# Scaling rows inside the transposition: the first stage of a hybrid recurrence and sparse-attention block

## The chip, the core and the metric

The kernel runs on one core of one Trainium2 chip. The metric is device time in microseconds (us) of one execution; lower is better. One execution was also recorded by the hardware profiler, and its trace gives every instruction of every engine with its start and length: TensorE (PE, with the loading of its stationary operand as PEld), VectorE (DVE), ScalarE (ACT), GpSimd (POOL), and SyncE (SP), which issues most transfers. L12 stands for line 12 of the kernel.

## The reference

One layer of a streaming encoder over 512 tokens of width 2048, in float32. Only the head of it matters here:

```python
h = rmsnorm(x, norm_w[layer])          # x: (1, 512, 2048)
proj = h @ w_in[layer]                 # w_in: (2048, IN_WIDTH), split into eleven parts
(a_q, a_f, a_i, a_g, c_q, c_kv, k_idx_raw, w_idx_raw, b_g, m_a, m_b) = jnp.split(proj, SPLIT_POINTS, axis=-1)
y_a = hgrn2_branch(a_q, a_f, a_i, a_g, ...)      # gated linear recurrence, 8 heads of 128
y_b = dsa_branch(c_q, c_kv, k_idx_raw, ...)      # sparse attention over chosen keys
merged = sigmoid(m_a) * (y_a @ w_pa) + sigmoid(m_b) * (y_b @ w_pb)
out = rmsnorm(x + merged @ w_out, final_norm_w)
```

rmsnorm(x, w) is x times 1 / sqrt(mean(x * x) + 1e-6) of its row, times w by column. The factor of a row is one number for each token; w gives one number for each of the 2048 features.

## The kernel before

Products of float32 matrices are made from three products of rounded parts: each operand is split into a high part (rounded by ScalarE to the type fp32r) and a low part (the rest, subtracted by VectorE or GpSimd), and high x high, low x high and high x low are accumulated in one bank of PSUM. Nearly all of the span is such products, in jobs that follow one another on TensorE. The first of them can only start when the normalised input stands in SBUF with features on the partitions and tokens along the free axis, as xh (high) and xl (low). To make these is the first stage, the function start(). It also computes 272 of the columns of proj straight away: 256 columns of a_i (kept as v) and the 16 of w_idx_raw (kept as widx).

The order of the work is written out by hand: each engine runs its instructions in the order in which the program issues them, and waits by semaphores. ScalarE, VectorE, GpSimd and TensorE each work through one queue; SP's queue issues the loads of x (two halves for each tile of 128 tokens), of four groups of weights (raw[0] to raw[3], 512 rows by 272 columns each), of small rows, and of the first two weight tiles of the next stage (load_ahead).

The stage handles four tiles t of 128 tokens, each in four groups g of four 128 x 128 blocks. The names:

- turn (L309): 16 transpositions of tile t on TensorE by an identity, four to a bank of PSUM, pt.
- square and rstd (L298, L302): ScalarE sums the squares of the row's two halves, VectorE adds them, ScalarE takes the root. on_diag (L305): VectorE takes the reciprocal, the row factor, and puts it on a diagonal, diag. square, rstd and on_diag of tile t + 1 run within the work on tile t.
- spread (L337): a float32 matmul of an all-ones matrix by diag brings the factor of each token onto all partitions; VectorE copies it to SBUF as r (rrow).
- weigh (L317, tile 0 alone): the four blocks of a bank times the feature's weight wc, to ys[g]; then scaled (L398) multiplies by r. For tiles 1 to 3, scaled (L348) does both in four instructions for a group.
- high (L321) rounds ys[g] to xh[g] on ScalarE; low (L324) subtracts it on VectorE, for odd groups of tiles 1 to 3 on GpSimd.
- w_high and w_low (L329, L332): the same two parts of the group's weights, wh and wl (fh, fl in the profile); the low part of the last group is made on GpSimd.
- project (L371): the 48 products of a tile, 128 x 128 by 128 x 272, group by group; the next tile's follow (L344: turn, spread, the rows' work) is issued in the middle, after group 1, and the copies to v and widx at the end. In the last tile, prep(0), which splits the next stage's first weights, stands there instead.

Before the first transposition, TensorE runs four float32 matmuls of ones (L292) into a bank that nobody reads, and the transposition of the feature weights nw.

Of the kernel before, what the change touches and what calls it, by code (L numbers as in the profile page):

```python
# [26 lines left out]
F32 = mybir.dt.float32  # L27
FR = mybir.dt.float32r
AF = mybir.ActivationFunctionType
OP = mybir.AluOpType  # L30
# [4 lines left out]
T, D = 512, 2048  # L35
# [15 lines left out]
def hybrid_block(ctx, tc, x, norm_w, w_in, lb_table, gnorm_a, q_norm_w, kv_norm_w, w_uq,  # L51
# [3 lines left out]
    V, A, G, PE, SP = nc.vector, nc.scalar, nc.gpsimd, nc.tensor, nc.sync  # L55
# [7 lines left out]
    mmp = ctx.enter_context(tc.tile_pool(name="mmp", bufs=4, space=PSUM))  # L63
# [4 lines left out]
    def bank(name):  # L68
        return sdp.tile([128, 512], F32, name=name, tag="sd")
# [10 lines left out]
    def mm(ps, l, r, first, last):  # L80
        PE.matmul(ps, l, r, start=first, stop=last, skip_group_check=True)  # L81
# [168 lines left out]
    def start():  # L250
        R.v0 = enter("v0")
        p0 = enter("p0", side="right")
        ident = p0.tile([128, 128], F32, name="ident")
        A.dma_start(ident, c_ident)
        HF = D // 2
        nw = p0.tile([16, 128], F32, name="nw")
        wc = p0.tile([128, 16], F32, name="wc")
        xs = [[p0.tile([128, HF], F32, name=f"x{t}{i}") for i in range(2)] for t in range(4)]
        ys = [p0.tile([128, 4, 128], F32, name=f"y{g}") for g in range(4)]
        diag = p0.tile([128, 128], F32, name="diag")  # L260
        sq = p0.tile([128, HF], mybir.dt.bfloat16, name="sq")
        st = p0.tile([128, 4, 4], F32, name="st")
        rows = p0.tile([128, 128], F32, name="rows")
        G.memset(rows, 1.0)
        G.tensor_copy(ones_r, rows)
        wh = [p0.tile([128, 4, 272], FR, name=f"fh{i}") for i in range(4)]
        wl = [p0.tile([128, 4, 272], FR, name=f"fl{i}") for i in range(4)]
        raw = [None] * 4

        def load_x(t):  # L270
            for i in range(2):
                SP.dma_start(xs[t][i], x2[t * 128:(t + 1) * 128, i * HF:(i + 1) * HF])

        def load_w(i):
            raw[i] = p0.tile([128, 4, 272], F32, name=f"fr{i}")
            for o, c0, c1 in ((0, 2048, 2304), (256, 4992, 5008)):
                SP.dma_start(raw[i][:, :, o:o + c1 - c0],
                             w_in[i * 512:(i + 1) * 512, c0:c1].rearrange("(k p) n -> p k n", p=128))
# [12 lines left out]
        for _ in range(4):  # L291
            PE.matmul(warm[:, 0:128], ones, ones, start=True, stop=True)  # L292
        G.memset(rows, 0.0)
        pw = mmp.tile([128, T], F32, name="acc")
        PE.transpose(pw[:, 0:16], nw, ident[0:16, 0:16])
        V.tensor_copy(wc, pw[:, 0:16])

        def square(t, i):  # L298
            A.activation(sq, xs[t][i], AF.Square, accum_out=st[:, t, i:i + 1])

        def rstd(t):
            V.tensor_add(st[:, t, 2:3], st[:, t, 0:1], st[:, t, 1:2])  # L302
            A.activation(st[:, t, 2:3], st[:, t, 2:3], AF.Sqrt, bias=eps, scale=1.0 / D)

        def on_diag(t):  # L305
            V.reciprocal(st[:, t, 3:4], st[:, t, 2:3])
            V.tensor_scalar(diag, ident, st[:, t, 3:4], None, op0=OP.mult)

        def turn(t, g):  # L309
            pt = bank("pt")  # L310
            for j in range(4):
                k = g * 4 + j
                PE.transpose(pt[:, j * 128:(j + 1) * 128],
                             xs[t][k // 8][:, (k % 8) * 128:(k % 8) * 128 + 128], ident)
            return pt

        def weigh(pt, g):  # L317
            V.tensor_tensor(ys[g], pt.rearrange("p (j t) -> p j t", j=4),
                            wc[:, g * 4:g * 4 + 4, None].to_broadcast([128, 4, 128]), op=OP.mult)

        def high(t, g):  # L321
            A.activation(xh[g][:, :, t * 128:t * 128 + 128], ys[g], AF.Copy)

        def low(t, g):  # L324
            o = slice(t * 128, t * 128 + 128)
            (G if t and g % 2 else V).tensor_tensor(xl[g][:, :, o], ys[g], xh[g][:, :, o].bitcast(F32),
                                                    op=OP.subtract)

        def w_high(i):  # L329
            A.activation(wh[i], raw[i], AF.Copy)  # L330

        def w_low(i, eng):  # L332
            eng.tensor_tensor(wl[i], raw[i], wh[i].bitcast(F32), op=OP.subtract)

        v = hg[0, "v"] = R.v0.tile([128, 4, 256], F32, name="hv")

        def spread():  # L337
            pr = mmp.tile([128, T], F32, name="acc")
            PE.matmul(pr[:, 0:128], ones, diag, start=True, stop=True)
            r = p0.tile([128, 128], F32, name="rrow", bufs=2)  # L340
            V.tensor_copy(r, pr[:, 0:128])
            return r

        def follow(t):  # L344
            pts = [turn(t, g) for g in range(4)]
            r = spread()

            def scaled(g):  # L348
                for j in range(4):
                    V.scalar_tensor_tensor(ys[g][:, j, :], pts[g][:, j * 128:j * 128 + 128],  # L350
                                           wc[:, g * 4 + j:g * 4 + j + 1], r, op0=OP.mult, op1=OP.mult)
                high(t, g)

            scaled(0)
            scaled(1)
            low(t, 0)
            if t < 3:
                square(t + 1, 0)
            scaled(2)
            low(t, 1)  # L360
            if t < 3:
                square(t + 1, 1)
            scaled(3)
            if t < 3:
                rstd(t + 1)
            low(t, 2)
            if t < 3:
                on_diag(t + 1)
            low(t, 3)

        def project(t):  # L371
            o = slice(t * 128, t * 128 + 128)
            acc = mmp.tile([128, T], F32, name="acc")
            for g in range(4):
                if g == 2:
                    if t < 3:
                        follow(t + 1)
                    else:
                        prep(0)
                for n, (xp, wp) in enumerate(((xh, wh), (xl, wh), (xh, wl))):  # L380
                    for k in range(4):
                        mm(acc[:, 0:272], xp[g][:, k, o], wp[g][:, k, :], g + n + k == 0,
                           g + n + k == 8)
            A.activation(v[:, t, :], acc[:, 0:256], AF.Copy)
            V.tensor_copy(widx[:, t, :], acc[:, 256:272])

        pts = [turn(0, g) for g in range(4)]
        weigh(pts[0], 0)
        weigh(pts[1], 1)
        square(0, 0)  # L390
        square(0, 1)
        rstd(0)
        on_diag(0)
        w_high(0)
        weigh(pts[2], 2)
        r = spread()

        def scaled(g):  # L398
            V.tensor_tensor(ys[g], ys[g], r[:, None, :].to_broadcast([128, 4, 128]), op=OP.mult)
            high(0, g)  # L400

        scaled(0)
        scaled(1)
        w_low(0, V)
        w_high(1)
        low(0, 0)
        weigh(pts[3], 3)
        square(1, 0)
        scaled(2)
        low(0, 1)  # L410
        scaled(3)
        w_low(1, V)
        w_high(2)
        w_low(2, V)
        square(1, 1)
        low(0, 2)
        rstd(1)
        low(0, 3)
        on_diag(1)
        w_high(3)  # L420
        w_low(3, G)
        SP.dma_start(rows[0:16], lb_table.rearrange("a (h d) -> (a h) d", d=128))
        SP.dma_start(rows[16:20], q_norm_w.rearrange("o (k d) -> (o k) d", d=128))
        SP.dma_start(rows[20:22], kv_norm_w.rearrange("o (k d) -> (o k) d", d=128))
        SP.dma_start(rows[22:23], kidx_norm_w)
        SP.dma_start(rows[23:24], kidx_norm_b)
        SP.dma_start(rows[24:25], gnorm_a)
        load_ahead()
        for t in range(4):
            project(t)  # L430
        pt = bank("pt")
        PE.transpose(pt[:, :128], rows, ident)
        V.tensor_copy(cols[:, 0:25], pt[:, :25])
        leave("p0")
# [1122 lines left out]
```

## Time and profile before

| | |
|---|---|
| Times of three runs | 1369.58, 1370.32, 1370.65 us; median 1370.32 |
| Profiled execution: its span, first to last instruction | 1368.3 us; its own time is not given apart, the median of the runs is 2.0 us above this span |
| TensorE busy | 1347.3 us, 98% of the span |
| VectorE, ScalarE, GpSimd busy | 1072.6, 656.8, 83.2 us |
| First stage, on TensorE | from 1.38 to 46.77 us |

A busy figure is the time in which the engine had at least one instruction under way. A line of the timeline gives the start, the time from the first start to the last end of the instructions merged in it, the engine, the line of the kernel, the operation, out<-in by the program's names, the shape, the count, and in brackets the idle time before it with what ended it. A line of the waits gives the engine that waited and for what, the total, how often, and the longest.

### The profile page before, as it was taken

Reading aid. Unit: us, or ns where it says so; the run is one execution under the profiler, and the core shown is the slowest. Engines: PE = TensorE matmul, PEld = TensorE weight load, DVE = VectorE, ACT = ScalarE, POOL = GpSimd, SP = SyncE. Lnnn points to the kernel's source line nnn. Section 1 sums busy time; section 2 is a strip of 40 time slices with the busy share of each in tenths; the row PEclk is TensorE's granted clock in tenths of the full one; section 3 lists DMA queues with packets and bytes.
Section 4 is the critical chain, followed back from the end, with each engine's and each line's share of the span. In section 5 each row is a group of like instructions: output and inputs, shape, how many; then the busy total and the mean of one; then the engine's idle time right before and its main releaser. Section 6 shows DMA issues by size and latency. Waiting matters only on the chain. (4 is left out here: it accounts for less than half of the span.)

```text
span 1368.3 us, 26815 instructions
## 1 busy us (share of the span) xinstructions
PE 1347.3 (98%) x10940; PEld 1250.0 (91%) x10940; DVE 1072.6 (78%) x1743; ACT 656.8 (48%) x1054; POOL 83.2 (6%) x85
## 2 busy tenths in 40 slices
PE   8999999999999999999999999999999999999997
PEld 7888999999999999998999788878888888899996
DVE  7896889988898888876779989675556658899856
ACT  6555445545544444546744343645534334354435
POOL 2100000000000000000030303050101100000000
PEclk9999999999999999999999999999999999999999
DMA  6334345544454445446235423434856556643554
GB/s 206 93 109 138 107 141 170 155 139 140 139 148 126 116 138 152 144 139 200 63 103 149 130 79 109 137 104 144 285 179 203 197 172 221 208 150 113 171 201 168
DMA packets 144734, 204.79 MB, mean 150 GB/s; under 512 B 10538, under 2 KB 85987, under 8 KB 144483
## 3 DMA queue, kind: packets, MB, share of 16 engines
q1 hardware_dynamic: 144322, 202.75, 47.6%
q8 instruction: 86, 1.41, 0.4%
q14 instruction: 38, 0.30, 0.1%
q10 hardware_dynamic: 288, 0.33, 0.1%
HBM read 167.89 MB, written 35.15 MB: 148 GB/s over the span
## 5 line engine op out<-in xcount | busy, mean ns | idle before, releaser
L150 ACT ACTIVATE bh<-wr 128x768 fp32r<-128x768 f32 x128 | 108.2, 845 | 218.7 <-issue 108.2
L152 ACT ACTIVATE wh<-sv 128x512 fp32r<-128x512 f32 x256 | 151.8, 623 | 84.7 <-DVE sv L145 65.5
L73 DVE TENSOR_TENSOR wl<-wr,wh 128x1024 fp32r<-128x1024 f32 (+1 forms) x104 | 127.9, 1231 | 60.7 <-ACT wh L72 60.4
L76 PE MATMUL pp<-s,wh 128*128 128x256 f32 x624 | 172.3, 276 | 0.0
L77 PE MATMUL pp<-s,wh 128*128 128x256 f32 x624 | 172.3, 276 | 0.0
L78 PE MATMUL pp<-s,wl 128*128 128x256 f32 x624 | 172.3, 276 | 0.0
L153 DVE TENSOR_TENSOR bl<-wr,bh 128x768 fp32r<-128x768 f32 x128 | 122.3, 955 | 51.3 <-ACT bh L150 51.1
L72 ACT ACTIVATE wh<-wr 128x1024 fp32r<-128x1024 f32 (+1 forms) x104 | 108.1, 1040 | 113.1 <-PE acc L77 60.0
L154 DVE TENSOR_TENSOR wl<-sv,wh 128x1024 fp32r<-128x1024 f32 x128 | 156.5, 1223 | 7.4 <-ACT wh L152 1.1
L76 PE MATMUL acc<-xh,wh 128*128 128x512 f32 x304 | 121.6, 400 | 0.0
L78 PE MATMUL acc<-xh,wl 128*128 128x512 f32 x304 | 118.6, 390 | 0.0
L77 PE MATMUL acc<-xl,wh 128*128 128x512 f32 x304 | 118.4, 390 | 0.0
L77 PEld LDWEIGHTS pp<-s,wh 128*128 128x128 f32 x624 | 117.2, 188 | 0.0
L76 PEld LDWEIGHTS pp<-s,wh 128*128 128x128 f32 x624 | 117.1, 188 | 0.0
L78 PEld LDWEIGHTS pp<-s,wl 128*128 128x128 f32 x624 | 117.1, 188 | 0.0
L76 PE MATMUL pp<-xh,bh 128*128 128x256 f32 x416 | 114.9, 276 | 0.0
L78 PE MATMUL pp<-xh,bl 128*128 128x256 f32 x416 | 114.9, 276 | 0.0
L77 PE MATMUL pp<-xl,bh 128*128 128x256 f32 x416 | 114.9, 276 | 0.0
L76 PE MATMUL acc<-yh,wh 128*128 128x512 f32 x256 | 100.2, 391 | 0.0
L78 PE MATMUL acc<-yh,wl 128*128 128x512 f32 x256 | 99.8, 390 | 0.0
L77 PE MATMUL acc<-yl,wh 128*128 128x512 f32 x256 | 99.7, 390 | 0.0
L145 DVE TENSOR_TENSOR sv<-wr 128x512 f32<-128x512 f32 x128 | 87.9, 687 | 9.2 <-DMA wr<-in_w_in_dram 5.9
(390 smaller groups left out, 3688.4 us busy)
## 6 DMA issues: line engine op xcount, KB each, us to landing
wr<-in_w_in_dram SPq DMA_DIRECT2D x136, 512.0 KB, 3.7
wr<-in_w_out_dram SPq DMA_DIRECT2D x32, 512.0 KB, 3.7
mg<-gate_d SPq DMA_DIRECT2D x48, 256.0 KB, 5.0
gate_d<-c SPq DMA_DIRECT2D x44, 256.0 KB, 5.2
wr<-in_w_in_dram SPq DMA_DIRECT2D x36, 256.0 KB, 2.9
wr<-in_w_pa_dram SPq DMA_DIRECT2D x16, 512.0 KB, 5.7
wr<-in_w_pb_dram SPq DMA_DIRECT2D x16, 512.0 KB, 4.2
x<-in_x_dram SPq DMA_DIRECT2D x8, 512.0 KB, 4.2
```

The lines of the kernel that those rows point to most:

```text
L72: A.activation(hi, src, AF.Copy)
L73: V.tensor_tensor(lo, src, hi.bitcast(F32), op=OP.subtract)
L76: PE.matmul(ps, lh, rh, start=first, stop=False, skip_group_check=True)
L77: PE.matmul(ps, lh, rl, start=False, stop=False, skip_group_check=True)
L78: PE.matmul(ps, ll, rh, start=False, stop=last, skip_group_check=True)
L145: V.tensor_tensor(sv[:, 0:2, :], b[:, 1:3, :], b[:, 0:1, :].to_broadcast([128, 2, 256]), op=OP.add)
L150: A.activation(bh, b[:, 1:4, :], AF.Copy)
L152: A.activation(vh[:, i:i + 2, :], sv[:, i:i + 2, :], AF.Copy)
L153: V.tensor_tensor(bl, b[:, 1:4, :], bh.bitcast(F32), op=OP.subtract)
L154: V.tensor_tensor(vl, sv, vh.bitcast(F32), op=OP.subtract)
```

## The change

- The row factor goes into the transposition. turn multiplies each block of x, as the stationary operand, by diag of its tile in a float32 matmul, where a transposition by the identity stood. spread, rrow and the scaled functions are gone; weigh alone (one VectorE instruction for a group) serves all tiles, followed by the rounding to xh. There are two diag tiles.
- As turn now needs diag, the squares and the root of tile 0 stand ahead of turn(0).
- Twenty-six more float32 matmuls of ones stand on TensorE ahead of turn(0).
- All low parts, of x and of the weights, are made on VectorE.
- project and follow are replaced by use(t, parts), which issues the products of the named groups (hh, lh, hl: high x high, low x high, high x low) and, when a tile's twelve are issued, its copies to v and widx, and by rows_of(t), which issues the rows' work. The products of tiles 0 and 1 are ordered by hand across the two tiles.
- On ScalarE, w_high(2) and w_high(3) now come after the squares and the root of tile 1; on VectorE, w_low(2) and w_low(3) come after rows_of(1).

```diff
-        diag = p0.tile([128, 128], F32, name="diag")
+        diag = [p0.tile([128, 128], F32, name=f"diag{i}") for i in range(2)]
...
+        for _ in range(26):
+            PE.matmul(warm[:, 0:128], ones, ones, start=True, stop=True)
...
-            V.tensor_scalar(diag, ident, st[:, t, 3:4], None, op0=OP.mult)
+            V.tensor_scalar(diag[t % 2], ident, st[:, t, 3:4], None, op0=OP.mult)
+
+        pts, accs, done = {}, {}, {}
+
+        def turn(t):
+            for g in range(4):
+                pts[t, g] = bank("pt")
+                for j in range(4):
+                    k = g * 4 + j
+                    PE.matmul(pts[t, g][:, j * 128:(j + 1) * 128],
+                              xs[t][k // 8][:, (k % 8) * 128:(k % 8) * 128 + 128], diag[t % 2],
+                              start=j == 0, stop=True, skip_group_check=True)
+
+        def weigh(t, g):
+            V.tensor_tensor(ys[g], pts.pop((t, g)).rearrange("p (j t) -> p j t", j=4),
                             wc[:, g * 4:g * 4 + 4, None].to_broadcast([128, 4, 128]), op=OP.mult)
             A.activation(xh[g][:, :, t * 128:t * 128 + 128], ys[g], AF.Copy)
...
-            (G if t and g % 2 else V).tensor_tensor(xl[g][:, :, o], ys[g], xh[g][:, :, o].bitcast(F32),
-                                                    op=OP.subtract)
+            V.tensor_tensor(xl[g][:, :, o], ys[g], xh[g][:, :, o].bitcast(F32), op=OP.subtract)
...
+        def use(t, *parts):
+            if t not in accs:
+                accs[t], done[t] = mmp.tile([128, T], F32, name="acc"), 0
+            o = slice(t * 128, t * 128 + 128)
+            for kind, g in parts:
+                xp, wp = {"hh": (xh, wh), "lh": (xl, wh), "hl": (xh, wl)}[kind]
+                for k in range(4):
+                    mm(accs[t][:, 0:272], xp[g][:, k, o], wp[g][:, k, :], done[t] == 0 and k == 0, done[t] == 11)
+                done[t] += 1
+            if done[t] == 12:
+                A.activation(v[:, t, :], accs[t][:, 0:256], AF.Copy)
+                V.tensor_copy(widx[:, t, :], accs[t][:, 256:272])
+
+        def rows_of(t):
+            weigh(t, 0)
+            weigh(t, 1)
             low(t, 0)
             if t < 3:
                 square(t + 1, 0)
+            weigh(t, 2)
             low(t, 1)
             if t < 3:
                 square(t + 1, 1)
+            weigh(t, 3)
             if t < 3:
                 rstd(t + 1)
             low(t, 2)
             if t < 3:
                 on_diag(t + 1)
             low(t, 3)
...
         square(0, 0)
         square(0, 1)
         rstd(0)
         on_diag(0)
         w_high(0)
+        turn(0)
+        weigh(0, 0)
+        weigh(0, 1)
         w_high(1)
         low(0, 0)
+        weigh(0, 2)
+        low(0, 1)
+        weigh(0, 3)
         square(1, 0)
         square(1, 1)
         low(0, 2)
+        low(0, 3)
+        w_low(0)
         rstd(1)
         on_diag(1)
+        w_low(1)
+        w_high(2)
         w_high(3)
+        use(0, ("hh", 0), ("hh", 1), ("lh", 0), ("hh", 2), ("lh", 1), ("hh", 3), ("lh", 2), ("lh", 3))
+        turn(1)
+        use(0, ("hl", 0), ("hl", 1))
+        rows_of(1)
+        w_low(2)
+        w_low(3)
...
         load_ahead()
-        for t in range(4):
-            project(t)
+        use(1, ("hh", 0), ("hh", 1), ("lh", 0), ("hl", 0), ("hh", 2), ("lh", 1), ("hl", 1), ("hh", 3), ("lh", 2),
+            ("lh", 3))
+        turn(2)
+        use(0, ("hl", 2), ("hl", 3))
+        use(1, ("hl", 2), ("hl", 3))
+        rows_of(2)
+        for t in (2, 3):
+            use(t, *((kind, g) for g in (0, 1) for kind in ("hh", "lh", "hl")))
+            if t == 2:
+                turn(3)
+                rows_of(3)
+            else:
+                prep(0)
+            use(t, *((kind, g) for g in (2, 3) for kind in ("hh", "lh", "hl")))
```

More of the change, by code (lines that the diff above doesn't have):

```diff
@@ L306, in on_diag @@
             V.reciprocal(st[:, t, 3:4], st[:, t, 2:3])
[L307 to L318, printed above, removed]
+            V.tensor_scalar(diag[t % 2], ident, st[:, t, 3:4], None, op0=OP.mult)
[10 more added lines that the diff above has]
+            V.tensor_tensor(ys[g], pts.pop((t, g)).rearrange("p (j t) -> p j t", j=4),
                             wc[:, g * 4:g * 4 + 4, None].to_broadcast([128, 4, 128]), op=OP.mult)
-        def high(t, g):
             A.activation(xh[g][:, :, t * 128:t * 128 + 128], ys[g], AF.Copy)
@@ L325, in low, with w_low @@
             o = slice(t * 128, t * 128 + 128)
-            (G if t and g % 2 else V).tensor_tensor(xl[g][:, :, o], ys[g], xh[g][:, :, o].bitcast(F32),
-                                                    op=OP.subtract)
+            V.tensor_tensor(xl[g][:, :, o], ys[g], xh[g][:, :, o].bitcast(F32), op=OP.subtract)
         def w_high(i):
             A.activation(wh[i], raw[i], AF.Copy)
-        def w_low(i, eng):
-            eng.tensor_tensor(wl[i], raw[i], wh[i].bitcast(F32), op=OP.subtract)
+        def w_low(i):
+            V.tensor_tensor(wl[i], raw[i], wh[i].bitcast(F32), op=OP.subtract)
         v = hg[0, "v"] = R.v0.tile([128, 4, 256], F32, name="hv")
[L337 to L355, printed above, removed]
+        def use(t, *parts):
[13 more added lines that the diff above has]
+            weigh(t, 1)
             low(t, 0)
@@ L358, in follow @@
                 square(t + 1, 0)
-            scaled(2)
+            weigh(t, 2)
             low(t, 1)
@@ L369, in follow @@
             low(t, 3)
[L371 to L389, printed above, removed]
         square(0, 0)
@@ L394, in start @@
         w_high(0)
[L395 to L404, printed above, removed]
+        turn(0)
+        weigh(0, 0)
+        weigh(0, 1)
         w_high(1)
         low(0, 0)
-        weigh(pts[3], 3)
+        weigh(0, 2)
+        low(0, 1)
+        weigh(0, 3)
         square(1, 0)
[L409 to L414, printed above, removed]
         square(1, 1)
         low(0, 2)
+        low(0, 3)
+        w_low(0)
         rstd(1)
-        low(0, 3)
         on_diag(1)
+        w_low(1)
+        w_high(2)
         w_high(3)
-        w_low(3, G)
+        use(0, ("hh", 0), ("hh", 1), ("lh", 0), ("hh", 2), ("lh", 1), ("hh", 3), ("lh", 2), ("lh", 3))
[4 more added lines that the diff above has]
+        w_low(3)
         SP.dma_start(rows[0:16], lb_table.rearrange("a (h d) -> (a h) d", d=128))
```

1 line of the change is left out of this document (removed).

## The prediction

> **What bounds the kernel now.** I read the page first (span, clock line), then the busy time by stages, then who waited for whom on TensorE, then the first 50 us as a timeline, engine by engine.
>
> ```profile
> span 1368.3 us, 26815 instructions
> ...
> PEclk9999999999999999999999999999999999999999
> ```
>
> The stretches up to and after the first stage (start:end, length, then busy us and count of TensorE, its weight loads, VectorE, ScalarE, GpSimd):
>
> ```profile
> 0.00:46.80 46.80, 40.45 (x275) 38.34 (x275) 34.49 (x91) 26.74 (x47) 11.35 (x15) 1.00 0.46 152
> 46.80:1360.00 1313.20, 1306.79 (x10669) 1211.65 (x10666) 1035.55 (x1646) 626.86 (x1000) 71.86 (x70) 1.00 0.48 149
> ```
>
> From 46.8 to 1360 TensorE stands still for 1313.2 - 1306.8 = 6.4 us in all; in the first stage alone it is 46.8 - 40.5 = 6.4 us too. So what TensorE loses or wins before the second stage moves the end almost one for one. The 6.4 us behind could soak up a delay only if they hung on the clock on the wall; they hang on the other engines, whose work moves along with TensorE's.
>
> The first stage on TensorE (start, duration, line, operation, count, idle before and its releaser), and its transpositions as a group (shortest, median and longest in ns):
>
> ```profile
> 1.38 2.08 PE L292 MATMUL warm<-ones_r 128*128 128x128 f32 x8 [1.38 <-POOL ones_r L265]
> ...
> 5.43 3.67 PE L313 MATMUL pt<-ident,x 128*128 128x128 f32 x16 [1.75 <-DMA x<-in_x_dram]
> ...
> 11.65 1.28 PE L81 MATMUL acc<-fh,xh 128*128 128x272 f32 x4 [1.77 <-ACT xh L322]
> 13.40 1.27 PE L81 MATMUL acc<-fh,xl 128*128 128x272 f32 x4 [0.47 <-DVE xl L326]
> ...
> 16.29 1.11 PE L81 MATMUL acc<-fh,xl 128*128 128x272 f32 x4
> 17.20 0.81 PE L81 MATMUL acc<-fl,xh 128*128 128x272 f32 x4
> 17.85 1.91 PE L313 MATMUL pt<-ident,x 128*128 128x128 f32 x16
> ...
> 21.80 0.67 PE L81 MATMUL acc<-fl,xh 128*128 128x272 f32 x4
> 22.31 0.67 PE L81 MATMUL acc<-fh,xh 128*128 128x272 f32 x4
> ...
> 28.89 0.49 PE L339 MATMUL acc<-diag,ones_r 128*128 128x128 f32 x2
> 29.13 0.75 PE L81 MATMUL acc<-fh,xh 128*128 128x272 f32 x4
> ...
> 46.77 0.27 PE L432 MATMUL pt<-ident,rows 128*128 128x128 f32 x1
> ```
>
> ```profile
> L313 PE MATMUL pt<-ident,x x64: 270/273/472, 5.4 to 36.9; 128*128 128x128 f32 x64
> ```
>
> The stage ends at 46.77. The clock line shows full speed in every slice, but the rows do not agree for the first 17 us: 16 transpositions take 3.67 us at 5.43 and 1.91 us at 17.85, four products 1.11 us apart from their start at 16.29 (0.91 to the next four) and 0.50 us (21.80 to 22.31) later. So TensorE runs at half rate until about 17.5. Less the tail of the last one, a pass over 128 columns costs (3.67 - 0.47) / 15 = 0.213 us at half rate and (1.91 - 0.27) / 15 = 0.109 at full; a product of 272 columns costs 0.227 and 0.125. And what counts below: a float32 matmul is two passes (four in the code are x8 in L292, one is x2 in L339), a transposition one (16 are x16).
>
> **Where the change's first work starts.** turn(0) now multiplies by diag[0] and so needs the factor of the first tile, not only x.
>
> ```profile
> 8.22 0.29 ACT L303 ACTIVATE st<-st,cols 128x1 f32<-128x1 f32 x1 [0.31 <-DVE st L302]
> 8.55 0.16 DVE L306 RECIPROCAL st<-st 128x1 f32<-128x1 f32 x1 [0.36 <-ACT st L303]
> 8.75 0.29 DVE L307 TENSOR_SCALAR diag<-ident,st 128x128 f32<-128x128 f32 x1
> ```
>
> diag[0] is there at 9.04. But 26 more warm matmuls, 52 passes, stand ahead of it from about 3.6. When does the clock rise under them? In the trace it rose at about 17.5, after products without a break since 13.40 (4.1 us), or since 11.65 with one of 0.47 (5.9 us). Counted from 1.38 that is 5.5 to 7.3. At 5.5, 8.9 passes have run at 0.213 and 43.1 follow at 0.109, to 10.2; at 7.3 the sum is 11.1. I take the middle, 10.7: the warm matmuls, not diag, set the start, 1.7 us after diag is ready.
>
> **TensorE's work from there.** Four turns of 16 matmuls, 32 passes each: 4 x 32 x 0.109 = 14.0 us, where transpositions cost 4 x 16 x 0.109. No row shows such matmuls in a stream at full rate; from below, 0.109 a pass is the transposition's own rate with the same x as weights; from above, the single pair at 28.89 takes 0.24 until the next starts, 1.4 us more over 64. I take 0.109, as the stream is the nearer row. 192 products at 0.125 are 24.1. spread (four times that pair) goes. So 38.0 us of work at full rate: without a wait the stage would end at 10.7 + 38.0 = 48.7, already 1.9 later than now: full rate in the first 17 us does not quite pay for 64 doubled passes and a start at 10.7.
>
> **The waits.** Durations for the other engines:
>
> ```profile
> 13.12 1.04 ACT L299 ACTIVATE sq<-x 128x1024 bf16<-128x1024 f32 x1
> 14.06 0.18 ACT L299 ACTIVATION_READ_ACCUMULATOR sq<-x 128x1 f32 x1
> ...
> 15.79 0.63 ACT L322 ACTIVATE xh<-y 128x512 fp32r<-128x512 f32 x1 [0.57 <-DVE y L399]
> 16.32 1.09 ACT L330 ACTIVATE fh<-fr 128x1088 fp32r<-128x1088 f32 x1
> ```
>
> ```profile
> 11.46 1.28 DVE L333 TENSOR_TENSOR fl<-fr,fh 128x1088 fp32r<-128x1088 f32 x1
> 12.66 0.69 DVE L326 TENSOR_TENSOR xl<-y,xh 128x512 fp32r<-128x512 f32 x1
> 13.27 0.68 DVE L318 TENSOR_TENSOR y<-pt,wc 128x512 f32<-128x512 f32 x1
> ...
> 21.32 2.16 DVE L350 SCALAR_TENSOR_TENSOR y<-pt,wc,rrow 128x128 f32<-128x128 f32 x8
> ...
> 27.76 1.07 DVE L307 TENSOR_SCALAR diag<-ident,st 128x128 f32<-128x128 f32 x1
> ```
>
> In a queue the next operation starts some 0.1 us before the end of the one ahead (xh at 15.79, fh at 16.32; xl at 12.66, y at 13.27), so a weigh or low costs VectorE 0.60, a rounding of xh 0.53, of fh 1.0, a square with its read 1.1; a small operation 0.16 (the reciprocal at 8.55), a handover between engines 0.04 (8.22 + 0.29 to 8.55).
>
> First wait, at ("hh", 2) of tile 0. It needs wh[2], and w_high(2) now stands on ScalarE behind rstd(1), thus behind both squares of tile 1. Starting at 10.7: bank 0 of turn(0) is full 0.87 + 0.17 later, weigh(0, 0) ends at 12.5, xh of group 0 at 13.2, of group 1 at 14.0, w_high(1) runs 13.9 to 15.0, xh of groups 2 and 3 to 16.4, the squares to 18.6, the add on VectorE at 18.6 (its lows and w_low(0) are done by 18.3), the root 18.8 to 19.1, w_high(2) 19.0 to 20.1. TensorE ends turn(0) at 14.2, waits 0.36 for wh[1] and has ("hh", 0), ("hh", 1), ("lh", 0) done at 16.1. It stands from 16.1 to 20.2: 4.1 us. No transfer sets this: squares of tile 1 ran at 13.1 and a w_high(2) at 16.3 in the rows above, with nothing waited for, so their inputs had landed. From 20.2 it has lh 1, hh 3, lh 2, lh 3, turn(1), hl 0 and hl 1, to 27.2, and the parts of tile 1 without a wait, since rows_of(1) overlaps turn(1) (its last low, 30.7, is ahead of ("lh", 3) at 31.7). diag[2] at 30.0 is in time for turn(2) at 32.2.
>
> Second wait, after turn(2). The parts ("hl", 2), ("hl", 3) of tiles 0 and 1 come next; each completes an accumulator, so use puts the copies to v and widx into the queues of ScalarE and VectorE, ahead of rows_of(2). The weigh of tile 2 thus waits for TensorE's last product of tile 1 (37.7), though its banks are full from 33. After it: widx 0.16, weigh to 38.7, xh to 39.3; ("hh", 0) of tile 2 starts at 39.4, 1.7 us late, and ("lh", 0) another 0.2.
>
> Third wait, at turn(3). The late rows_of(2) makes diag[3] late too: squares on ScalarE to 42.6, root at 43.1, reciprocal 43.4, diag ready at 43.9, while TensorE is through groups 0 and 1 of tile 2 at 42.6: 1.3 us. If diag costs 1.07, as at 27.76 beside GpSimd's work, 0.8 more; that work is gone, so I take 0.29.
>
> **The other parts, all beside TensorE.** The sixteen scalar_tensor_tensor of a tile (8 in 2.16) become four weighs, 4.2 to 2.4 us; two lows come over from GpSimd (+1.2), w_low(3) as well (+1.2): VectorE's total hardly moves. Their cover: wl[3] is ready at 33.0, needed at 36.3; without these 3.3 us, w_low(3) would cost up to 1.28. SP's queue issues the same transfers in the same order (rows and load_ahead come later in the text only); they wait on nothing that moves: 0. prep(0) stays behind TensorE's group 1 of tile 3, and ScalarE and VectorE come to it longer ahead of TensorE's need than now: 0.
>
> **Sum.** 10.7 + 38.0 + (0.36 + 4.07 + 1.71 + 0.23 + 1.34 = 7.7) = 56.4, against 46.8: 9.6 us later. The profiled span becomes 1377.9. The median of the runs shown is 1370.3, 2.0 above the span (what lies around it), so 1379.9. Bounds of this case: -0.5 and -0.8 (clock early, waits a tenth shorter), +0.4, +1.4 and +0.8 (clock late, passes, diag): 1378.6 to 1382.
>
> **Rivals.**
> (a) TensorE's clock falls back in the wait of 4.1 us.
>
> ```profile
> PE sc L76 <- ACT relu L655: 2.4, 2, 1.6
> ```
>
> Warm, the longest stand in the trace is 1.6 us (last figure; the row is from who waited for whom), so nothing there excludes it. It would cost 4.1 to 5.9 us of products at 0.227 for 0.125, 1.8 to 2.6 us: 1381.7 to 1382.5. [...]
> (b) The products wait for nothing: the order fills TensorE, and work alone sets the end, 48.7: 1372.2, within 0.2% (2.7 us, about what a measurement of this kernel can tell from no change), so not slower. It holds if ScalarE has wh[2] by 16.1 and not 20.1. For it: of the 6.4 us that TensorE stands in the stage now, 1.4 + 1.75 + 1.77 + 0.47 lie before 13.4, so a full queue has kept it fed afterwards. Against it: the root of tile 1 sits ahead of w_high(2) in one queue, and there is no other queue for it.
> (c) The first wait alone is away (w_high(2) early, the rest as forecast): 4.1 less, 1375.8.
> [...]
>
> **How the numbers follow.** Forecast 0.66, (a) 0.12, (c) 0.09, (b) 0.06, (d) 0.03, another delay 0.02, faster by something unseen 0.02 (no term of the sum gains so much). The range 1375.5 to 1383 takes in the forecast, (a) and (c), 0.87 together less their tails. Slower 0.66 + 0.12 + 0.09 + 0.03 + 0.02 = 0.92, same 0.06, faster 0.02.
>
> **What would show it.** In the profile after: the 60 warm passes ending near 10.7 with the rate doubling at 5.5 to 7.3; each turn about 3.5 us; TensorE idle before a product with xh or fh at about 16 for 4 us, released by ScalarE's fh; idle of 1.7 us ahead of tile 2's first product, with weigh of tile 2 released by TensorE and not earlier than the widx copies; idle before the last turn released by diag; the rows transposition (L432 now) near 56. Wrong if that lies below 50, if w_high(2) runs ahead of the root, or if TensorE's later waits shrink by what the stage lost.

## The result and the profile after

The changed kernel takes 1382.28 us (median of four runs, 1381.32 to 1382.62), the kernel before beside it 1370.49 us: ratio 1.0086, 95% interval 1.0074 to 1.0099, so 11.8 us slower. The profiled execution took 1381.32 us, with a span of 1379.5 us.

The stretches up to and after the first stage, after the change (columns as in the prediction; the last three figures are the granted clock, the busy share of the DMA engines and GB/s):

```profile
0.00:58.40 58.40, 50.07 (x381) 48.78 (x382) 29.67 (x55) 27.54 (x48) 0.94 (x8) 0.97 0.40 131
58.40:1371.30 1312.90, 1306.75 (x10669) 1212.06 (x10667) 1035.00 (x1646) 626.68 (x999) 72.22 (x70) 1.00 0.47 149
```

Behind the first stage nothing changed: 1312.90 us with TensorE busy for 1306.75, against 1313.20 and 1306.79. All of the loss lies in the first 58.4 us. TensorE stands for 58.4 - 50.1 = 8.3 us there, 2 us more than before (46.8 - 40.5 = 6.4); the rest is longer work.

TensorE's timeline in that stage:

```profile
3.60 7.13 PE L298 MATMUL warm<-ones_r 128*128 128x128 f32 x52
10.57 3.74 PE L318 MATMUL pt<-diag,x 128*128 128x128 f32 x32
...
15.57 0.66 PE L81 MATMUL acc<-fh,xl 128*128 128x272 f32 x4
20.11 1.27 PE L81 MATMUL acc<-fh,xh 128*128 128x272 f32 x4 [3.88 <-ACT fh L332]
21.18 1.11 PE L81 MATMUL acc<-fh,xl 128*128 128x272 f32 x4
22.09 1.04 PE L81 MATMUL acc<-fh,xh 128*128 128x272 f32 x4
...
23.98 3.73 PE L318 MATMUL pt<-diag,x 128*128 128x128 f32 x32
27.47 1.25 PE L81 MATMUL acc<-fl,xh 128*128 128x272 f32 x8
...
37.08 2.26 PE L81 MATMUL acc<-fl,xh 128*128 128x272 f32 x16
41.28 0.76 PE L81 MATMUL acc<-fh,xh 128*128 128x272 f32 x4 [1.94 <-ACT xh L325]
...
44.12 0.66 PE L81 MATMUL acc<-fl,xh 128*128 128x272 f32 x4
45.76 3.81 PE L318 MATMUL pt<-diag,x 128*128 128x128 f32 x32 [0.97 <-issue]
...
58.41 0.27 PE L421 MATMUL pt<-ident,rows 128*128 128x128 f32 x1
```

The transposition of rows, which ended the stage at 46.77 before, starts at 58.41: 11.64 us later. Three stands are new: 3.88 us for the high part of a weight (fh), 1.94 us for the high part of x of tile 2, 0.97 us ahead of turn(3). And four products that take 0.50 us at full rate take 0.91 after the first stand (21.18 to 22.09). The stretch in which the profile's clock records are low, with its length, TensorE's busy time and count, and the last three figures as above:

```profile
19.52:22.93 3.41, 2.82 (x12) 0.50 0.45 144
```

What the stands wait for is in the queues of ScalarE and VectorE:

```profile
18.77 0.29 ACT L305 ACTIVATE st<-st,cols 128x1 f32<-128x1 f32 x1 [0.23 <-DVE st L304]
18.97 2.09 ACT L332 ACTIVATE fh<-fr 128x1088 fp32r<-128x1088 f32 x2
```

```profile
39.80 0.17 DVE L350 COPY widx<-acc 128x16 f32<-128x16 f32 x1 [0.83 <-ACT hv L349]
39.89 1.28 DVE L323 TENSOR_TENSOR y<-pt,wc 128x512 f32<-128x512 f32 x2
...
45.37 0.29 DVE L309 TENSOR_SCALAR diag<-ident,st 128x128 f32<-128x128 f32 x1
```

w_high(2) and w_high(3) run at 18.97, right behind the root of tile 1, as the program has them. weigh of tile 2 starts at 39.89, right behind the copy of widx, which waits for ScalarE's copy of v and so for the last products of tile 1. diag[3] is ready at 45.66 and turn(3) starts 0.1 later.

### The profile page after: what moved, and what is told of

It reads as the page before. It is cut to its first block, busy times and chain, and to the rows that moved or that the text cites. A ratio compares the mean times of both kernels' runs of the same rounds, so it can differ in the third digit from the quotient of the medians.

```text
span 1379.5 us, 26987 instructions
## 1 busy us (share of the span) xinstructions
PE 1356.8 (98%) x11048; PEld 1260.8 (91%) x11048; DVE 1067.2 (77%) x1706; ACT 657.3 (48%) x1054; POOL 73.2 (5%) x78
```

## The experiments

My theory: TensorE's own work and its waits in this stage set the time one for one, and the waits come from the order in ScalarE's and VectorE's queues. The rivals were that waits only move to the next place, that the doubled passes or VectorE's load are the cause, and that the clock costs more than the waits. Every kernel ran beside the kernel before on one chip; the ratio is always to it.

### The order, in two moves

e_early: the high parts of the last two weights go ahead of the squares of tile 1.

```diff
         weigh(0, 3)
+        w_high(2)
+        w_high(3)
         square(1, 0)
...
         w_low(1)
-        w_high(2)
-        w_high(3)
         use(0, ("hh", 0), ("hh", 1), ("lh", 0), ("hh", 2), ("lh", 1), ("hh", 3), ("lh", 2), ("lh", 3))
```

> Edit: w_high(2) and w_high(3) stand ahead of the squares of tile 1 on ScalarE. Theory (ScalarE's order makes the first wait): TensorE's wait at (hh, 2) of tile 0 shrinks from 3.9 to about 1.3 us and is too short for the clock to fall back; the squares come 2 us later, so a new wait of about 1.6 us for diag[1] appears ahead of turn(1). The first stage ends near 56.2 instead of 58.4; time about 2.2 us less than the changed kernel's 1382.3, near 1380. Rival (the wait is for the landing of the third weight group, not for the queue): (hh, 2) still starts near 20, the stage still ends near 58.4 and the time stays at 1382.

Measured: 1380.11 us, ratio 1.0072 (1.0059 to 1.0085). TensorE in its profile:

```profile
18.31 0.78 PE L81 MATMUL acc<-fh,xh 128*128 128x272 f32 x4 [1.13 <-ACT fh L332]
22.62 3.81 PE L318 MATMUL pt<-diag,x 128*128 128x128 f32 x32 [1.53 <-issue]
57.12 0.28 PE L421 MATMUL pt<-ident,rows 128*128 128x128 f32 x1
```

The stand shrinks from 3.88 to 1.13, the products behind it run at full rate (four in 0.50, 18.92 to 19.42), and 1.53 us come back ahead of turn(1), whose diagonal is now the later one. The stage ends 1.3 earlier although turn(0) began 0.9 later in this run (11.51). So the order in ScalarE's queue makes the first stand, and part of the gain moves.

e_rows: the rows' work of tile 2 goes ahead of the products that close tiles 0 and 1.

```diff
         turn(2)
+        rows_of(2)
         use(0, ("hl", 2), ("hl", 3))
         use(1, ("hl", 2), ("hl", 3))
-        rows_of(2)
```

> Edit: rows_of(2) is issued ahead of the last parts of tiles 0 and 1, so that the copies to v and widx stand behind it. Theory (those copies make the second and third waits): the 1.9 us ahead of tile 2's first product, the 0.2 after it and the 1.0 ahead of turn(3) all go, the stage ends near 55.0, time 3.3 us less, near 1379. Rival (TensorE would wait there anyway, for the rows' work itself): the weigh of tile 2 starts at once, but tile 2's first product waits for over 1 us all the same; time 1381 to 1382.

Measured: 1378.43 us, ratio 1.0060 (1.0046 to 1.0074). TensorE:

```profile
43.51 3.73 PE L318 MATMUL pt<-diag,x 128*128 128x128 f32 x32
...
56.14 0.27 PE L421 MATMUL pt<-ident,rows 128*128 128x128 f32 x1
```

The second and third stands are gone and nothing takes their place; the stage ends at 56.14 where 55.0 was expected, as turn(0) began 1.1 later in this run (11.65). Both hung on the copies to v and widx that stood ahead of rows_of(2).

e_both has the two diffs above together.

> The changed kernel with two moves of order: the high parts of the last two weights (w_high(2), w_high(3)) ahead of the squares of tile 1, and rows_of(2) ahead of the two use() calls that close tiles 0 and 1. Theory (the waits are the work of the order, and are independent of each other): the first wait falls from 4.0 to about 1.1, the two of 1.9 and 1.0 go or shrink, no fall of the clock; with turn(1) then waiting for its diagonal about 1.5, the stage ends 4 to 6 us earlier than the changed kernel's 58.4, at 52.5 to 54.5, time 1375.5 to 1378. Rival (waits only move: what isn't waited for at one place is waited for at the next): 56 or later, 1379 or more.

Measured: 1376.04 us, ratio 1.0042 (1.0028 to 1.0056, without one of the five executions, which took 7768.89 us). TensorE:

```profile
17.30 0.77 PE L81 MATMUL acc<-fh,xh 128*128 128x272 f32 x4 [1.12 <-ACT fh L332]
...
21.72 3.81 PE L318 MATMUL pt<-diag,x 128*128 128x128 f32 x32 [1.54 <-issue]
...
52.63 0.27 PE L421 MATMUL pt<-ident,rows 128*128 128x128 f32 x1
```

The stage ends 5.8 us earlier than in the changed kernel and the time is 6.2 us lower: half of the loss was order. The waits are independent, as the theory had it. What is left, 52.63 against 46.77, is TensorE's own work: it is busy for 48.43 us of the stage against 40.45, of which the doubled passes are 64 x 0.109 = 7.0, while it stands 2.1 us less than in the kernel before (1.54 and 1.12 are the longest stands behind turn(0)).

### The clock

e_fill puts 15 float32 matmuls of ones into the first stand, so that TensorE is busy while it waits.

```diff
-        use(0, ("hh", 0), ("hh", 1), ("lh", 0), ("hh", 2), ("lh", 1), ("hh", 3), ("lh", 2), ("lh", 3))
+        use(0, ("hh", 0), ("hh", 1), ("lh", 0))
+        for _ in range(15):
+            PE.matmul(warm[:, 0:128], ones, ones, start=True, stop=True)
+        use(0, ("hh", 2), ("lh", 1), ("hh", 3), ("lh", 2), ("lh", 3))
```

> Edit: 15 more float32 matmuls of ones stand between (lh, 0) and (hh, 2) of tile 0; 30 passes of 0.112 fill 3.35 of the 3.9 us in which TensorE stands still. Theory (the clock falls back because TensorE stands still): the products from 20.1 on run 0.125 apart at once, no stretch of half clock is recorded, the stage ends near 57.2 and the time is 1.2 us less, near 1381. Rival (those products are slow for another reason, or the clock is set by what ran before 16): they run 0.227 apart as before, the stage ends at 58.4 or later.

Measured: 1381.31 us, ratio 1.0083 (1.0069 to 1.0097). TensorE:

```profile
21.04 0.77 PE L81 MATMUL acc<-fh,xh 128*128 128x272 f32 x4 [0.53 <-ACT fh L332]
...
36.75 2.26 PE L81 MATMUL acc<-fl,xh 128*128 128x272 f32 x16
40.95 0.77 PE L81 MATMUL acc<-fh,xh 128*128 128x272 f32 x4 [1.94 <-ACT xh L325]
...
42.55 1.11 PE L81 MATMUL acc<-fl,xh 128*128 128x272 f32 x4
43.46 1.11 PE L81 MATMUL acc<-fh,xh 128*128 128x272 f32 x4
...
58.45 0.27 PE L424 MATMUL pt<-ident,rows 128*128 128x128 f32 x1
```

From 21.04 on, behind 0.53 us of standing in place of 3.88, the products run at full rate (four in 0.51, 21.64 to 22.15): half clock came with the long stand. The expected end of the stage (57.2), and a trace without half clock, missed: in this execution turn(0) began 0.9 later (11.50) and the clock fell later instead, at 41.94, behind the stand of 1.94 us (four products in 0.91 from 42.55). The clock records of the changed kernel hold 13.66 us at full clock (5.86 to 19.52) and 3.41 at half (19.52 to 22.93), four times and once 3.41, and I count e_fill in steps of 3.41 as well. Ahead of its fall lies 38.53 to 41.94: TensorE worked in it until 39.0 and from 40.95, and stood for 1.94. In the changed kernel the same stand of 1.94 us was followed by products at full rate (four in 0.50, 42.62 to 43.12); there a step ends at 40.00, with 0.66 us of standing ahead of it (36.58 to 40.00) and 1.29 behind it (40.00 to 43.41). So what differs between the two is where the stand lies against the steps, and that is not the same in every profile. The time hardly tells e_fill from the changed kernel; the conclusion rests on the rows.

Four steps of 3.41 us side by side, from the changed kernel, the kernel before, e_fill and e_best_pad (a kernel described below):

```profile
16.10:19.52 3.42, 0.14 (x2) 1.00 1.04 413
1358.95:1362.36 3.41, 1.14 (x10) 1.00 0.84 327
38.53:41.94 3.41, 1.47 (x10) 1.00 0.00 0
20.09:23.51 3.42, 1.57 (x14) 1.00 0.66 224
```

TensorE stood in them for 3.28, 2.27, 1.94 and 1.85 us. The first three were followed by half clock, the one of the kernel before behind the last of its matmuls:

```profile
1362.36:1365.78 3.42, 0.00 (x0) 0.50 0.85 325
```

The fourth was not. A stand of 3.9 us puts half of itself, 1.94 us, or more into one step of 3.41 wherever the steps lie, so by my estimate from these rows a fall was next to certain. The ends of the rows are modelled, and no experiment varied the length of a stand step by step.

### The doubled passes

e_transpose replaces the float32 matmul by a one-pass transposition with the same waits; diag holds ones in place of the factors, so the row factor is left out of the result.

```diff
-            V.tensor_scalar(diag[t % 2], ident, st[:, t, 3:4], None, op0=OP.mult)
+            V.tensor_scalar(diag[t % 2], ident, st[:, t, 3:4], 0.0, op0=OP.mult, op1=OP.is_gt)
...
-                    PE.matmul(pts[t, g][:, j * 128:(j + 1) * 128],
-                              xs[t][k // 8][:, (k % 8) * 128:(k % 8) * 128 + 128], diag[t % 2],
-                              start=j == 0, stop=True, skip_group_check=True)
+                    PE.transpose(pts[t, g][:, j * 128:(j + 1) * 128],
+                                 xs[t][k // 8][:, (k % 8) * 128:(k % 8) * 128 + 128], diag[t % 2])
```

> Edit: turn uses the one-pass transposition where the float32 matmul by diag stood; diag is made 0 and 1 by a comparison of the same operands at the same place, so every wait for it stays. The row factor is left out of the result. Theory (the second pass of each of 64 matmuls is on the path): a turn takes 1.75 instead of 3.57 us, four times 1.8 less 1.2 us that come back as longer waits: the stage ends near 52.4, the time is 6 us less, near 1376. Rival (the stage is paced by ScalarE and VectorE, and a shorter turn only lengthens the waits): the stage ends above 56.5 and the time is at most 2 us less.

Measured: 1381.25 us, ratio 1.0082 (1.0068 to 1.0096). The stage ends at 51.91, 6.5 earlier, as expected (turn(0) began 0.45 earlier, at 10.12). The time fell by only 1.0: the expectation of the time missed. What stood still later, from the waits and the timeline of TensorE:

```profile
PE hl L81 <- issue: 2.6, 2, 2.1
```

```profile
766.53 0.39 PE L81 MATMUL hl<-hq,hk 128*32 128x32 f32 x21 [0.58 <-issue]
...
828.46 0.64 PE L81 MATMUL hl<-hq,hk 128*32 128x32 f32 x50 [0.41 <-DVE hq L769]
831.16 0.43 PE L81 MATMUL hl<-hq,hk 128*32 128x32 f32 x14 [2.06 <-issue]
```

In the middle of a burst of 64 tiny products, the first 50 of which had waited 0.41 for their operand, TensorE stands 2.06 us for nothing that the profile shows ("issue"), and the clock falls behind it for 3.4 us (granted clock 0.67 from 831.2 to 836). This code was not touched. The page shows a queue of 86 transfers of 16 KB of instructions, and TensorE has 2 x 10984 instructions here (matmuls and weight loads): one transfer for each 255 (packets and MB of the queue):

```profile
q8 instruction: 86, 1.41, 0.4%
```

The transfers keep step with TensorE's work: in the changed kernel 84 of them fall between 34.6 and 1350.1 us, and TensorE starts 2 x 10721 instructions there, again 255 for each. The row at 766.53 is a shorter stand of the same sort. If each transfer is a block of some 255 of TensorE's instructions, 64 fewer of each kind ahead of the burst move the limits of the blocks by half a block against the code; that is my estimate from these counts. I formed the theory that the burst now runs across a limit faster than the next block comes in, and tested it.

e_pad is e_transpose with 128 more TensorE instructions at the start, so that by this count the blocks lie as in the changed kernel (the factor is left out here too).

```diff
-        for _ in range(26):
+        for _ in range(34):
+            PE.matmul(warm[0:32, 0:32], ones[:, 0:32], ones[:, 0:32], start=True, stop=True)
+        for _ in range(24):
             PE.matmul(warm[:, 0:128], ones, ones, start=True, stop=True)
```

> Edit: the kernel with one-pass transpositions (row factor left out, as there) with 34 tiny float32 matmuls (32 rows out, 32 columns) of ones and 24 instead of 26 full ones ahead of turn(0): 128 more instructions in TensorE's queue, as many as the change from two passes to one had taken out, for about 0.6 us of work before turn(0). Theory (TensorE's instructions are fetched in blocks of 16 KB; in the kernel without padding a block ends within a burst of tiny matmuls of the recurrence, where TensorE stood 2.1 us with nothing waited for): the blocks lie as in the changed kernel again, the stands of 0.6 and 2.1 us at 766 and 831 go, TensorE's time after the first stage is back from 1317.7 to 1312.5 to 1313.5, and the time falls by 3 to 5 us, to 1376 to 1378. Rival (the later stage loses because the rows' values or the earlier start changed it): the stands stay and the time stays at 1381 or rises by 0.6.

Measured: 1378.01 us, ratio 1.0058 (1.0045 to 1.0070), 3.2 less than e_transpose although its stage ended later (54.44). In this execution turn(0) began at 11.77, the half clock lasted two steps (18.28 to 25.11), and the granted clock was 0.95 elsewhere up to 159.7. The burst:

```profile
831.26 0.75 PE L81 MATMUL hl<-hq,hk 128*32 128x32 f32 x64 [0.53 <-DVE hq L771]
```

All 64 run in one go. From the end of the stage to the start of TensorE's last matmul it takes 1314.29 us, above the 1312.5 to 1313.5 expected; that is 1.7 more than in the changed kernel, and 1.4 of it arises by 160 us, under the lower clock.

e_pad alone also moves the start; where the stands lie says more. Counted from the start of the program, 6473 matmuls lie ahead of the stand at 766.53 in e_transpose, and as many ahead of stands of 0.75 in e_nowarm (774.01) and 0.87 in e_best2 (758.37), at three different places of the burst; 7238 lie ahead of the 2.06, and 7239 ahead of a stand of 1.35 in b_warm. Each of these five stands ended 1.2 to 1.5 us after a transfer of 16 KB of the instruction queue had landed. The same count does not always bring a stand: e_fill, e_nowarm, e_best and e_best2 run through a burst at the second of these places without a stand. So after an edit at the start there were stands of 0.58 to 2.06 us inside bursts at 758 to 831 us. That TensorE waits in them for its next instructions fits these counts and remains my theory: no row names what it waits for. Of the 5.1 us by which e_transpose's rest is longer than the changed kernel's (1317.74 against 1312.63), matched product by product, 0.7 arises at 641.5 (a wait for ScalarE, 1.29 where it was 0.61), 0.7 at the first stand, and 3.7 at the second and the half clock behind it. Why the wait at 641.5 is longer stays open.

### The warm matmuls

e_nowarm takes the 26 warm matmuls out of the changed kernel.

```diff
-        for _ in range(26):
-            PE.matmul(warm[:, 0:128], ones, ones, start=True, stop=True)
```

> Edit: the changed kernel without the 26 added warm matmuls. Theory (they cost 1.4 us of start and pay by the clock): turn(0) starts at 9.2 when diag[0] is ready instead of at 10.6, but at half rate, its banks fill 0.4 to 2 us later, ScalarE's chain and the first wait's end follow, and the stage ends 0.5 to 1.5 us later, near 59.5: 1383 to 1384. Rival (the start sets the rest of the stage): 1.4 us less, 1381.

Measured: 1383.66 us, ratio 1.0093 (1.0079 to 1.0106). TensorE:

```profile
9.46 6.12 PE L316 MATMUL pt<-diag,x 128*128 128x128 f32 x32 [5.79 <-DVE diag L307]
21.07 1.27 PE L81 MATMUL acc<-fh,xh 128*128 128x272 f32 x4 [3.98 <-ACT fh L330]
59.66 0.27 PE L419 MATMUL pt<-ident,rows 128*128 128x128 f32 x1
```

turn(0) starts 1.1 earlier and takes 2.4 longer, most of it at half rate; the stage ends 1.3 later. The warm matmuls are worth about 1.3 us to this order, as expected. Behind the stage 1.2 us more are lost, 0.75 of them in the stand at 774.01.

b_warm gives the kernel before 16 warm matmuls, eight ahead of the first transpositions and eight after the first spread.

```diff
         V.tensor_copy(wc, pw[:, 0:16])
+        for _ in range(8):
+            PE.matmul(warm[:, 0:128], ones, ones, start=True, stop=True)
...
         r = spread()
+        for _ in range(8):
+            PE.matmul(warm[:, 0:128], ones, ones, start=True, stop=True)
```

> The kernel before with one thing of the change added: eight products of ones ahead of the first transpositions and eight behind the product that spreads the factors, so that the clock rises earlier than 17.5 us. Theory (in the kernel before the first tile is paced by the loads and by VectorE, not by TensorE's rate): the stage still ends at 46.8 +-0.4 and the time is 1370 +-0.5. Rival (the half-rate start of the kernel before is worth its TensorE time): 2 to 3 us earlier, 1367.5 to 1368.5.

Measured: 1374.95 us, ratio 1.0036 (1.0024 to 1.0048): both expectations of the time missed. TensorE:

```profile
13.29 0.77 PE L81 MATMUL acc<-fh,xl 128*128 128x272 f32 x4 [0.98 <-DVE xl L328]
...
17.51 1.91 PE L315 MATMUL pt<-ident,x 128*128 128x128 f32 x16
...
46.63 0.27 PE L436 MATMUL pt<-ident,rows 128*128 128x128 f32 x1
...
823.42 0.74 PE L81 MATMUL hl<-hq,hk 128*32 128x32 f32 x63 [0.52 <-DVE hq L785]
825.52 0.22 PE L81 MATMUL hl<-hq,hk 128*32 128x32 f32 x1 [1.35 <-issue]
```

On the stage the theory holds: the products run at full rate (four in 0.50, 13.90 to 14.40), wait for VectorE instead, and turn(1) starts at 17.51 where it started at 17.85; the end moves by 0.14. A clock that is warm from the start is worth 0.14 us to the kernel before. The time got worse behind the stage, which takes 1316.84 us to TensorE's last instruction, against 1313.04: 3.8 more. The stand inside the burst is there again (1.35 us, ahead of the last of 64), as in e_transpose, with only warm matmuls added; another 0.73 at 64.2, for VectorE, and 0.42 at 1087.1 are new too; the remaining 1.3 us I have not located.

### The low parts

e_pool puts the low parts of odd groups and of the last weight back on GpSimd.

```diff
-            V.tensor_tensor(xl[g][:, :, o], ys[g], xh[g][:, :, o].bitcast(F32), op=OP.subtract)
+            (G if t and g % 2 else V).tensor_tensor(xl[g][:, :, o], ys[g], xh[g][:, :, o].bitcast(F32), op=OP.subtract)
...
-            V.tensor_tensor(wl[i], raw[i], wh[i].bitcast(F32), op=OP.subtract)
+            (G if i == 3 else V).tensor_tensor(wl[i], raw[i], wh[i].bitcast(F32), op=OP.subtract)
```

> The changed kernel with one part undone: the low parts of odd index of tiles 1 to 3 and that of the last weight are put back on GpSimd. Theory (VectorE's load is not what sets this stage: TensorE is busy or waits for ScalarE): no gain; the first wait is unchanged (near 3.9), the one in front of turn(3) grows by 0.5 to 1 where GpSimd works beside VectorE, time 1381.5 to 1383.5. Rival (VectorE, loaded with all low parts, is late for the products): the waits behind turn(1) go and the time is 1379.5 to 1380.5.

Measured: 1383.19 us, ratio 1.0095 (1.0082 to 1.0109), not to be told from the changed kernel by its time. Its stage ends at 60.33, 1.9 later, of which 0.9 is a later turn(0) (11.44). In the trace turn(3) waits 1.76 in place of 0.97, because diag[3] takes 1.06 beside GpSimd's subtraction (at 46.17) and 0.29 without:

```profile
47.68 3.81 PE L318 MATMUL pt<-diag,x 128*128 128x128 f32 x32 [1.76 <-issue]
46.52 1.06 DVE L309 TENSOR_SCALAR diag<-ident,st 128x128 f32<-128x128 f32 x1
```

So this part of the change costs nothing and saves about 0.8 us; VectorE's load is not the cause of the loss.

### A version that beats both

e_best keeps the float32 matmul for tile 0 alone. For the others VectorE scales x in place and TensorE transposes in one pass; the order of the stage is written anew, and the low parts of the last two weights are on GpSimd. Of its long diff the core:

```diff
+        def scale(t, i):
+            V.tensor_scalar(xs[t][i], xs[t][i], st[:, t, 3:4], None, op0=OP.mult)
...
+                if t == 0:
+                    PE.matmul(pts[t, g][:, j * 128:(j + 1) * 128], block, diag,
...
+                else:
+                    PE.transpose(pts[t, g][:, j * 128:(j + 1) * 128], block, ident)
...
+            (G if i in (2, 3) else V).tensor_tensor(wl[i], raw[i], wh[i].bitcast(F32), op=OP.subtract)
```

> Edit: tiles 1 to 3 have their rows scaled in place on VectorE (two tensor_scalar, 1024 columns each) and are then turned by one-pass transpositions; tile 0 keeps the matmul by diag; the whole stage is ordered again by the traces' durations, so that ScalarE has the squares of tile 1 and wh[2], wh[3] early and the copies to v and widx stand behind the rows' work; w_low(2), w_low(3) on GpSimd; 20 warm matmuls. Theory: TensorE's work from 9.4 is 3.6 + 48 x 0.109 + 24.1 = 33 us, with 1 to 2 us of waits the stage ends at 43.6 to 44.5 against the 46.8 of the kernel before. By the count of its instructions the blocks lie differently from both kernels (98 instructions on from the kernel before), so if code blocks matter the part after the stage may lose up to 5 us: 1368 to 1373. Rival (blocks do not matter): 1367 to 1368.

Measured: 1371.55 us, ratio 1.0007 (0.9999 to 1.0016): the stage ended at 47.29, not at 43.6 to 44.5; that expectation missed, and the time lies in the expected 1368 to 1373 for another reason. VectorE, and GpSimd beside it:

```profile
15.83 0.75 DVE L316 TENSOR_SCALAR x<-x,st 128x1024 f32<-128x1024 f32 x1
...
17.69 2.98 DVE L316 TENSOR_SCALAR x<-x,st 128x1024 f32<-128x1024 f32 x1
```

```profile
16.73 6.33 POOL L346 TENSOR_TENSOR fl<-fr,fh 128x1088 fp32r<-128x1088 f32 x2 [15.14 <-ACT fh L343]
```

The same scaling takes 0.75 us alone and 2.98 beside GpSimd's subtraction, and turn(1) stood 1.97 us for it.

e_best_pad is e_best with the 34 tiny matmuls of e_pad and 16 warm ones, to lay the blocks as in the changed kernel by the count above.

> Edit: the reordered kernel with 34 tiny matmuls and 16 warm ones instead of 20, 120 more instructions in TensorE's queue, so that its blocks lie as in the changed kernel (218 on from the kernel before). Theory: the stage ends at 43.6 to 44.5 and the part after it takes as long as in the changed kernel and in the kernel before: 1367 to 1368, 2 to 3 us below the kernel before. Rival (something else than the blocks slows the part after an early stage): 1370 or more.

Measured: 1371.67 us, ratio 1.0006 (0.9997 to 1.0016). Its stage ended 1.1 later (48.41) and the rest was 1.1 shorter (1312.73 against 1313.79): nothing won. The part behind the stage came out as expected, the stage and the time did not.

e_best2 takes GpSimd out and orders the queues for that, two changes at once. Of its diff against e_best the first line:

```diff
-            (G if i in (2, 3) else V).tensor_tensor(wl[i], raw[i], wh[i].bitcast(F32), op=OP.subtract)
+            V.tensor_tensor(wl[i], raw[i], wh[i].bitcast(F32), op=OP.subtract)
```

> The version meant to beat both kernels, without GpSimd: tile 0 is still transposed and scaled by one fp32 product with the diagonal, tiles 1 to 3 are scaled in place by VectorE (two instructions of 0.75 us a tile) and then transposed in one pass; all low parts are on VectorE; the order of the whole stage is written anew, so that every product is issued after its operands. 20 products warm the clock. Theory (the first stage is TensorE's own work plus its waits, and everything behind it moves with its end): about 10.8 + 32.3 of work + 0.7 of waits, so the stage ends near 43.8 us, 3.0 before the kernel before, time 1367.5 (1366.5 to 1369). Rival (the collision of GpSimd with VectorE was not what held the version before this one at 47.3; it is the scaling on VectorE in front of each transposition): the wait for x stays near 2 us, the stage ends at 46 or later and the time is 1370 or above.

Measured: 1367.67 us, ratio 0.9982 (0.9974 to 0.9991), 2.6 us (0.2%) faster than the kernel before, as expected; how much of the gain over e_best is the order and how much GpSimd is not shown. TensorE:

```profile
9.37 3.74 PE L326 MATMUL pt<-diag,x 128*128 128x128 f32 x32
...
16.54 1.91 PE L329 MATMUL pt<-ident,x 128*128 128x128 f32 x16
...
43.45 0.27 PE L530 MATMUL pt<-ident,rows 128*128 128x128 f32 x1
...
758.37 0.40 PE L81 MATMUL hl<-hq,hk 128*32 128x32 f32 x25 [0.87 <-issue]
```

After 9.37 TensorE waits 0.27 and 0.29 us in the whole stage, and it ends 3.3 us before that of the kernel before. Behind it 0.87 us are lost again inside a burst of the tiny products.

## Why the prediction came out as it did

The forecast was 1379.9 us, from a stage that ends at 56.4. It ended at 58.41, and the time was 2.4 above the forecast: above the bounds that its own terms gave (1378.6 to 1382), inside the range because that took in rival (a). Its steps, each with what the profile after shows:

- The start of turn(0): 10.7 forecast, 10.57 measured, with the clock rising at 5.86 (forecast 5.5 to 7.3). Right, but by luck within a spread: the rise lay between 4.9 (e_transpose) and 8.1 (e_rows) in the profiles with the same warm matmuls, and turn(0) began between 10.1 and 11.7 in them.
- Two passes of 0.109 for each float32 matmul: the turn at 23.98 gives way to products at 27.47, 3.49 us for 32 passes. Right. The 0.03 of rival (d) stood for four passes in place of two: no run shows that, and the runs showed these two.
- The first stand: 4.07 forecast, 20.11 - 15.57 - 0.50 = 4.04 measured, released by fh behind the root. Right in place, size and cause (e_early).
- The second: 1.71 and 0.23 forecast. Measured 41.28 - 37.08 - 2.00 = 2.20, 0.23 and a restart of 0.1: 0.6 more. Right in cause (e_rows); too short, since the copy of widx came only after ScalarE's copy of v (0.83 of waiting for hv in the row at 39.80), 0.4 after the product, where I had counted the copy of widx alone.
- The third: 1.34 forecast, 45.76 - 44.12 - 0.50 = 1.14 measured; diag at 0.29, as taken. Right (e_rows, e_pool).
- The end of the stage moves the time one for one: the stage 11.64 later, the span 11.2, the time 11.8. Right for this change. It is not a law: in e_transpose and b_warm the code behind the stage lost 5.1 and 3.8 us, the stands inside the bursts being the largest part that was located.

The step that failed is rival (a). I gave a fall of the clock in the stand of 4.1 us a chance of 0.12, and no run shows a ground for so low a chance. The longest stand between products of the kernel before, 1.6 us, left it open, and behind the last of its matmuls its clock did fall, 2.27 us after they ended (the rows under "The clock"). The fall came in the changed kernel, and in all six profiles with a stand of 3.9 to 4.1 us: the changed kernel, e_rows, e_pool, e_transpose, e_pad and e_nowarm. In e_fill 1.94 us of one step came ahead of a fall too. Its price was over-stated, 1.8 to 2.6 us, while the 20 products from 20.11 to 23.98 took 3.87 in place of 2.50: 1.37. Half speed lasted 3.41 us in all (6.83 in e_pad, where TensorE stood for 2.48 us of the first slow step too), and 0.6 of it passed before the first product. With 1.4 for the clock and 0.6 for the second stand the forecast's 56.4 becomes 58.4. That the time fell where rival (a) had put it, 1381.7 to 1382.5, is in part luck: the clock cost less than (a) charged, and the second stand made up for it.

Rivals (b) and (c), no waits or all but the first, are out by the rows. The argument that full rate in the first 17 us does not pay for the doubled passes holds: the kernel before has no use for that rate (b_warm), and one-pass transpositions move the stage by 6.5 us (e_transpose).

## What to carry to other kernels

In a stage that TensorE fills, list for each product which queue makes its last operand and what stands ahead of it there; here three moved lines were worth half of the loss. Price a long stand of TensorE with the half-rate products behind it: about 1.4 us here behind 3.88 us, with a fall also where 1.94 us of a step of 3.41 were stood (e_fill). And where a shorter start does not shorten the whole, look for "issue" stands in bursts of tiny products far behind: here 2.06 us (e_transpose) and 1.35 (b_warm) came with a changed count of instructions at the start.

## What the runs showed of the hardware

- The start is not the same in every profile: with the same 52 warm passes, full speed came between 4.90 (e_transpose) and 8.11 us (e_rows), and turn(0) began at 10.12 and 11.65.
- Half clock came behind steps of 3.41 us in which TensorE had stood for 3.28 us (the changed kernel), 2.48 (e_pad), 2.27 (the kernel before, at its end) and 1.94 (e_fill), and not behind one with 1.85 (e_best_pad).
- TensorE stood for 2.06 us (e_transpose) and 1.35 us (b_warm) inside a burst of 64 products that takes 0.75 us without a stand (e_pad), behind 7238 and 7239 matmuls, released by nothing that the profile shows; the first was gone when 128 instructions at the start were added (e_pad).
- VectorE's instructions took longer beside GpSimd's: the scaling of 128 x 1024 took 2.98 us in place of 0.75 (e_best), diag of 128 x 128 1.06 in place of 0.29 (e_pool).
